# Five instead of four of the eight row pairs of the gate products by seven products, two of them with three sums of weights made in memory

## The chip, the cores and the metric

The kernel runs on one core of one Trainium2 chip. The metric is the device time of one execution in microseconds (us); the time of a kernel is the median of its runs. A run is profiled separately, and the profile's times come from that one execution. Engines are named as in the profile: PE is the matrix engine, PEld its weight loads, DVE the vector engine, ACT the scalar engine, POOL the GpSimd engine, SP the engine that issues most transfers.

## The reference

One layer of an encoder over 256 tokens of width 2048, in float32:

```python
h = rms_norm(x, attn_norm)
proj = h @ w_in
qa, ka, va, qb, kb, vb, ga, gb = jnp.split(proj, split_points, axis=-1)
ya = windowed_gqa(qa, ka, va, table, sink_a)
yb = dilated_attention(qb, kb, vb, table)
merged = sigmoid(ga) * (ya @ w_branch_a) + sigmoid(gb) * (yb @ w_branch_b)
x = x + merged @ w_out
hf = rms_norm(x, ffn_norm)
x = x + (gelu(dwconv(hf @ w_ffn_gate)) * (hf @ w_ffn_up)) @ w_ffn_down
x = x + sigmoid(rms_norm(x, ple_norm) @ w_ple_gate) * (p @ w_ple_proj)
return rms_norm(x, final_norm)
```

What matters here are `ga` and `gb`, the two gates: each is 256 tokens x 2048 columns, from 2048 rows of `w_in`. All products are made to nearly float32 exactness: every operand is split into a high and a low part of a shorter float type, and a product is three products (high x high, high x low, low x high).

## The kernel before, in words

**Blocks and pieces.** All weights are cut into 128 x 128 blocks and laid in memory in the order in which they are used (`_stream`), 16 blocks to a piece, 8 blocks (512 KB) to a load. SP issues the loads into six buffers called `raw` (L255). ACT copies a load to its high part `whi` (L278), DVE subtracts to get the low part `wlo` (L279). There are four buffers of each, so the splits run at most four ahead of PE.

**Jobs.** `_plan` lists the jobs in order: projections of the heads with the attention between them, then the gates in four quarters of the columns, then the output projection (`o`), the wide middle part (`g`, `u`, `d0`, `d1`) and the last gate (`pp`, `pgs`, `pg`). The first quarter of the gates is made plainly (`ga`, `gb`). The other three are jobs of the kind `gab`, here called gab 1, 2 and 3: each makes a quarter of `ga` and the same quarter of `gb` together, 256 tokens x 1024 columns, summing over 16 row blocks. The 16 row blocks are taken as eight pairs, 0 to 7.

**Plain pairs and pairs by seven products.** A pair is a 2 x 2 by 2 x 2 product of big blocks (two halves of the tokens, two row blocks, two groups of four column blocks). Done plainly it takes 8 products, each of three PE passes of 512 columns: 24 matmuls. Done by seven products (`seven_product`, the pairs in the second value of `_pairs`) it takes 7 x 3 = 21, but needs sums of weights and sums of the input. A plain pair is split in two parts of 8 blocks; a pair by seven products in four parts: b22 (4 blocks), two sums (8 blocks, tile `sums`), b11 and b12 (8), b22 and a third sum t4 (8). On DVE such a pair has a `wlo` of 512 elements, three of 1024, and two additions: t2 = b11 + first sum (L287), t4 = b12 + t2 (L289). A "whole" pair (`_whole`) gets its t2 ready-made from memory instead, and leaves out L287.

**Sums made in memory.** The two sums (and for a whole pair the third) of the gate and output pairs are made before their use by POOL's transfers from memory to memory, some of them adding on the way (`sums_in_memory`): for a plain set one copy of 512 KB and two additions of 256 KB (L324, L328, L329); for a whole set another copy (L327) and, after a wait, another addition (L331). `MADE_AT` lists at which job each set is asked for; POOL takes them in that order, and waits between the copies and the additions. `back` loads a set's two sums into one of two buffers `sums` (L344): the first two at job `bb` 0, each later one as soon as the split of the sums of the pair two before is done. The third sum is loaded behind the weights into the second half of a `raw` buffer (L264).

**Sums of the input.** `sums_of_input` makes the four sums of the normed input that a pair needs (ACT and DVE, `add_up`), ahead of the gab jobs.

**What sets the order.** A helper records every operation and a scheduler sets the order on each engine; `keep` pins some. `at(i, f)` ties work to a step of a job.

Of the kernel before, what the change touches and what calls it, by code (L numbers as in the profile page):

```python
# [11 lines left out]
FR = mybir.dt.float32r  # L12
# [4 lines left out]
P = 128  # L17
T = 256
D = 2048
KC = D // P  # L20
# [17 lines left out]
SUB = 8  # L38
# [81 lines left out]


TOGETHER = 3
AHEAD = 8 + 3 * 4
SAVED = 8
SPLIT = 4
ROWS = 7
SHL = 6
LATER = 4
WHOLE = (2, 3, 6, 7)
GATED = (1, 2, 3, 5)  # L130
MADE_AT = [*range(11, 34, 2), 34, 35, 36, 37, 38, 40, 42, 45]


def _pairs(kind, c):

    if kind == "pgs":
        return [0, 1, 4, 5, 2, 6, 7, 3], range(4, 8)
    if kind == "gab":
        return [0, 4, 1, 2, 6, 3, 5, 7], GATED
    if kind == "o":  # L140
        return ([2, 4, 5, 6, 7, 0, 1, 3] if c else [0, 1, 2, 4, 5, 6, 7, 3]), range(LATER, LATER + 4)
    if kind == "d1" and c == 1:
        return [5, 0, 1, 6, 2, 3, 7, 4, 8, 9, 10], range(5)
    return [8, 0, 1, 2, 3, 9, 4, 5, 6, 7, 10], range(SAVED)
# [10 lines left out]
def _stream():  # L155

    blocks = [(j[2], j[4] + k, j[3]) for k in range(KC) for j in _JOBS[:FIRST]]
    for kind, half, name, n, k0, count in _JOBS[FIRST:]:
        if isinstance(n, tuple) and len(n) == 8:
            order, seven = _pairs(kind, half)  # L160
            _EIGHT.update(range(len(blocks), len(blocks) + KC * len(order), PIECE))
            for m in order:
                if m in seven:
                    _SEVEN.append(len(blocks))
                each = [(2 * m + 1, n[4:] + n[:4]), (2 * m, n)] if m in seven else [(2 * m, n), (2 * m + 1, n)]
                blocks += [(name, k0 + k, c) for k, cs in each for c in cs]
            continue
        if kind == "gg":
            blocks += [(name, k, c) for h in range(0, KC, SUB) for c in n for k in range(h, h + SUB)]
            continue  # L170
        blocks += [(name, k, c) for k in range(k0, k0 + count) for c in (n if isinstance(n, tuple) else (n,))]
    return blocks
# [3 lines left out]
_BLOCKS = _stream()  # L176
# [4 lines left out]
def _whole(a):  # L181

    if _BLOCKS[a][0] == "w_in":
        return False
    return _BLOCKS[a][0] in ("w_out", "w_ple_gate") or (_BLOCKS[a + SUB][1] % FHALF) // 2 in WHOLE


# [19 lines left out]
def _encoder(ctx: ExitStack, tc, xt, pt, cols, table, onehot, mask, ident_in, last_gain, wts, xrows, out):  # L207
# [38 lines left out]
    held = {}  # L246
# [86 lines left out]
    def early_row():  # L333
        return ap_.tile([P, W4], F32, name="row", tag="qf", bufs=4)
# [66 lines left out]
    def wide_product(i, still, n, w, tag, places=HALVES, late=0):  # L401

        accs = [ps.tile([P, W4], F32, name="acc", tag=tag, bufs=3 if tag == "acc" else 2) for _ in places]

        def step(k, t, hi, lo):
            xh, xl = (still(k)[:, c:c + T][:, places[t]] for c in (0, T))
            acc = accs[t][:, :w * P]  # L410
            nc.tensor.matmul(acc, xh, hi, start=(k == 0), stop=False)  # L411
            nc.tensor.matmul(acc, xh, lo, start=False, stop=False)  # L412
            nc.tensor.matmul(acc, xl, hi, start=False, stop=(k == n - 1 - t * late))  # L413

        later = []
        for k in range(n):
            run_due(i, k)
            b = state["at"]
            s, o = _SUB_OF[b]
            split_to(s + 3)  # L420
            hi, lo = (m[:, o:o + w, :] for m in subs[s])
            step(k, 0, hi, lo)
            if k < n - late:
                step(k, 1, hi, lo)
            else:
                later.append((k, 1, hi, lo))
            state["at"] = b + w
            if o == _SUBS[s][1] - w:
                del subs[s]
        def rest(side=None):  # L430
            acc, c = (accs[1][:, :T], 0) if side is None else (side, T // P)
            for e, (k, t, hi, lo) in enumerate(later):
                xh, xl = (still(k)[:, c:c + T][:, places[t]] for c in (0, T))
                for i, (xs, ws) in enumerate(((xh, hi), (xh, lo), (xl, hi))):
                    nc.tensor.matmul(acc, xs, ws[:, c:c + T // P, :], start=(side is not None and e + i == 0),  # L435
                                     stop=(e + i == len(later) + 1), skip_group_check=True)
        return accs, rest
# [133 lines left out]
    def at(i, f, *a):  # L571

        due.setdefault(i, []).append((f, a))
# [7 lines left out]
    ap_ = att.enter_context(tc.tile_pool(name="att", bufs=2))  # L581
# [66 lines left out]
    b = ps.tile([NH, 2 * T], F32, name="misc")  # L648
# [222 lines left out]
    def sums_of_input(e):  # L871

        m = GATED[e]
        two = early_row().rearrange("p (k t) -> p k t", t=T)
        for k in range(2):
            nc.scalar.activation(two[:, k, :], x[:, 2 * m + k, :], AF.Copy, scale=gain(0, 2 * m + k))
        add_up(two, of_input(m))

    def of_input(m):
        e = SPLIT + 2 * GATED.index(m)  # L880
        return [held["merged"][1][:, e + c, :].rearrange("p (b n) -> p b n", n=P) for c in range(2)]

    def combined(bank, th):
# [17 lines left out]
    def row():  # L901
        return held["ff"].tile([P, W4], F32, name="row", bufs=ROWS)
# [187 lines left out]
    for i, job in enumerate(_JOBS):  # L1090
        kind, n, _, _, _, blocks = job
# [23 lines left out]

        if i in MADE_AT:
            at((i, 2), sums_in_memory, MADE_AT.index(i))
        if kind == "gab" and n > 1:
            for e in range(2):
                at((i, 5 + 6 * e), sums_in_memory, len(_SEVEN) - 4 + 2 * (n - 2) + e)  # L1120
        if kind in ("gb", "ba") and n == 0:
            for e in range(2):
                at((i, 3 + 3 * e + 5 * (kind == "gb")), sums_of_input, 2 * (kind == "ba") + e)
        if kind == "bb" and n == 0:
            for e in range(2):
                at((i, 0), back)
        if kind == "gab":
# [2 lines left out]
        if kind == "gg":  # L1130
            held["asked"] = AHEAD
        if kind == "gg" or (kind == "g" and n == FHALF):
# [60 lines left out]
        if kind == "v":  # L1193
            far = n[0] >= KVH + HG
            acc, _ = wide_product(i, stills["v"], blocks, len(n), "acc", TWINS if far else HALVES)
        elif kind in ("o", "d0", "d1", "gab", "pgs"):
            names = ("p2", "p3", "p4", "c22"), ("p1", "p5", "p6", "p7")
            places = ("sp", "sp", "pt", "pt"), ("acc", "acc", "acc", "misc")
            tags = {a: b for e in range(2) for a, b in zip(names[e], places[e ^ (n != 3 if kind == "gab" else n)])}
            still, sums_at = {"o": (stills["o"], early), "gab": (stills["ga"], of_input), "pgs": (stills["pg"], of_residual)}.get(  # L1200
                kind, (lambda k: held["act"][:, k, :], shl))
            if kind == "gab":
                if n < QUARTERS - 1:
                    th = ap_.tile([P, 2, 2, W4], F32, name="th", tag="v", bufs=1)
                    held["th", n] = {"ga": [th[:, 0, t] for t in range(2)], "gb": [th[:, 1, t] for t in range(2)]}
                else:
                    th = ap_.tile([P, 2, W4], F32, name="th", tag="s3", bufs=1)
                    held["th", n] = {"ga": [th[:, t] for t in range(2)],
                                     "gb": [ap_.tile([P, W4], F32, name="th", tag="s1", bufs=2) for t in range(2)]}
            th = held.get(("th", "pp" if kind == "pgs" else n))  # L1210
            end = kind != "d0" and n == 1
            acc = seven_product(i, *_pairs(kind, n), still, lambda m, e: [a[:, e, :] for a in sums_at(m)], tags,
                                (lambda bank: combined(bank, th)) if kind in ("gab", "pgs") else
                                (lambda bank: spread_sums(n, bank, end)))
        elif kind in stills:
            tag = {"pg": ("acc", "pt"), "pp": ("sp", "acc"), "gb": ("sp", "sp"), "ga": ("acc", "acc"),
                   "ba": ("acc", "sp" if n == 1 else "acc"), "bb": ("sp", "pt" if n == 1 else "acc")}[kind][n % 2]
            acc, rest = wide_product(i, stills[kind], blocks, 4, tag, late=8 if last else 0)
        elif kind == "gg":
            acc = products_by_halves(i, movers["g"])  # L1220
        else:
            acc = product(i, movers[kind], blocks)
# [24 lines left out]
        elif kind in ("o", "d0", "d1"):  # L1247
            parts = held["ss1" if kind == "o" else "ss2"]
            for name, t, c in (("p2", 0, 0), ("p3", 0, 1), ("p4", 1, 0), ("c22", 1, 1)):
                if end:  # L1250
                    joined(2 * n + c, t, acc[name], parts)
                else:
                    a = row()
# [63 lines left out]
```

## Time and profile before

| what | value |
|---|---|
| median of three runs | 1453.88 us (1453.02 to 1455.77) |
| the profiled execution's own time | 1452.42 us |
| its span from the first to the last instruction | 1450.6 us |
| PE busy | 1438.0 us, 99% |
| DVE busy | 1164.3 us, 80% |
| ACT busy | 852.3 us, 59% |
| gab 1, gab 2, gab 3 on PE | 368.4 to 410.9, 427.4 to 469.1, 469.1 to 509.9 us |
| POOL makes the 24 sets of sums in memory | 62.6 to about 419 us |
| the output projection `o` begins | about 543 us |

How it is read: the page's first part gives busy times; a matmul's duration in it is that of a pipelined instruction, longer than the distance between two of them. Idle time of an engine that PE doesn't wait for costs nothing. "idle before <-releaser" names what ended a wait.

### The profile page before, as it was taken

The numbers are of one execution on the slowest core, as the hardware profiler recorded it, in microseconds if no ns is written. First come the engines' busy times: TensorE is split into PE (matmuls) and PEld (weight loads), VectorE is DVE, ScalarE is ACT, GpSimd is POOL, SyncE is SP. The second block draws the span as 40 slices with busy tenths as digits, with TensorE's granted clock in tenths as the row PEclk, the third lists the DMA queues.
The fourth block names the chain that finished last, engine by engine and source line by source line (L and its number), as shares of the span: only waits on it lengthen the run. The fifth ranks groups of instructions, "written<-read, shape, count | busy, mean of one in ns | idle before, by whom it ended". The sixth has DMA issues, their size and how long they took to land.

```text
span 1450.6 us, 20823 instructions
## 1 busy us (share of the span) xinstructions
PE 1438.0 (99%) x7483; PEld 1233.8 (85%) x7483; DVE 1164.3 (80%) x1678; ACT 852.3 (59%) x1212; POOL 159.1 (11%) x242
## 2 busy tenths in 40 slices
PE   9999999999999999999999999999999999999997
PEld 8888888888888888888888888888888888888886
DVE  7687665674788878879888878997889886988895
ACT  7465544454556656666555556775555555666864
POOL 0111111211110000201111100102111100010000
PEclk9999999999999999999999999999999999999999
DMA  9799999999987668968888896989888885798672
GB/s 325 252 262 258 255 267 255 272 273 289 267 297 249 209 215 264 299 237 284 295 303 277 290 331 224 283 286 314 288 302 293 283 312 168 256 297 280 215 240 87
DMA packets 124084, 386.30 MB, mean 266 GB/s; under 512 B 14148, under 2 KB 19268, under 8 KB 123852
## 3 DMA queue, kind: packets, MB, share of 16 engines
q1 hardware_dynamic: 91932, 298.44, 60.2%
q0 software_dynamic: 30032, 82.59, 22.4%
q10 hardware_dynamic: 2016, 3.94, 1.0%
q8 instruction: 58, 0.95, 0.3%
q14 instruction: 46, 0.38, 0.1%
HBM read 354.46 MB, written 52.47 MB: 281 GB/s over the span
## 4 chain that ended last, share of the span: by engine, by line
PE 97%; DMA 1%; DVE 1%; ACT 0%; issue 0%; SPq 0%; POOLq 0%; DVEq 0%; ACTq 0%
PE acc L383 29%; PE acc L386 15%; PE acc L463 10%; PE acc L464 10%; PE acc L462 10%; PE acc L411 5%; PE acc L413 5%; PE acc L412 5%; PE first L360 2%; DMA raw<-in_wts 1%; PE pt L949 1%; PE pt L735 0%; PE acc L435 0%; ACT whi L278 0%; DVE wlo L279 0%
## 5 line engine op out<-in xcount | busy, mean ns | idle before, releaser
L279 DVE TENSOR_TENSOR wlo<-raw,whi 128x1024 fp32r<-128x1024 f32 (+2 forms) x572 | 657.0, 1165 | 124.3 <-ACT whi L278 117.8
L278 ACT ACTIVATE whi<-raw 128x1024 fp32r<-128x1024 f32 (+2 forms) x572 | 569.6, 1012 | 258.0 <-PE acc L464 86.7
L383 PE MATMUL acc<-mov,whi 128*128 128x512 f32 x1840 | 441.6, 391 | 0.0
L383 PEld LDWEIGHTS acc<-mov,whi 128*128 128x128 f32 x1840 | 337.9, 188 | 65.4
L386 PEld LDWEIGHTS acc<-mov,wlo 128*128 128x128 f32 x1840 | 237.3, 191 | 9.1 <-ACT mov L516 0.2
L386 PE MATMUL acc<-mov,wlo 128*128 128x256 f32 x1840 | 242.8, 283 | 0.0
L500 ACT ACTIVATE t<-acc 128x256 f32<-128x256 f32 x115 | 43.6, 379 | 121.3 <-PE acc L383 121.3
L411 PE MATMUL acc<-whi,mov 128*128 128x512 f32 (+1 forms) x248 | 93.6, 377 | 0.0
L413 PE MATMUL acc<-whi,mov 128*128 128x512 f32 (+1 forms) x248 | 93.5, 377 | 0.0
L412 PE MATMUL acc<-wlo,mov 128*128 128x512 f32 (+1 forms) x248 | 93.5, 377 | 0.0
L504 DVE TENSOR_TENSOR u<-acc,t 128x256 f32<-128x256 f32 x100 | 42.1, 421 | 58.4 <-ACT t L500 58.2
L462 PE MATMUL acc<-whi,act 128*128 128x512 f32 x207 | 80.8, 391 | 0.2 <-ACT whi L278 0.2
L463 PE MATMUL acc<-wlo,act 128*128 128x512 f32 x207 | 80.6, 389 | 0.0
L464 PE MATMUL acc<-whi,act 128*128 128x512 f32 x207 | 80.6, 389 | 0.0
L908 POOL DMA_DIRECT2D x<-row x36 | 30.9, 873 | 451.1 <-DMA sums<-kept 160.4
L279 DVE TENSOR_TENSOR wlo<-sums,whi 128x1024 fp32r<-128x1024 f32 x53 | 64.6, 1219 | 12.1 <-ACT whi L278 12.0
L463 PE MATMUL acc<-wlo,mov 128*128 128x512 f32 x176 | 68.5, 389 | 0.0
L464 PE MATMUL acc<-whi,mov 128*128 128x512 f32 x176 | 68.5, 389 | 0.0
L462 PE MATMUL acc<-whi,mov 128*128 128x512 f32 x176 | 68.2, 390 | 0.0
L278 ACT ACTIVATE whi<-sums 128x1024 fp32r<-128x1024 f32 x53 | 55.9, 1056 | 16.1 <-PE acc L464 9.4
L411 PEld LDWEIGHTS acc<-whi,mov 128*128 128x128 f32 x248 | 47.0, 190 | 8.7 <-DVE first L504 0.5
L413 PEld LDWEIGHTS acc<-whi,mov 128*128 128x128 f32 x248 | 47.0, 190 | 8.5
(253 smaller groups left out, 2073.2 us busy)
## 6 DMA issues: line engine op xcount, KB each, us to landing
raw<-in_wts SPq DMA_DIRECT2D x461, 512.0 KB, 5.9
sums<-kept SPq DMA_DIRECT2D x53, 512.0 KB, 5.3
kept<-in_wts POOLq DMA_DIRECT2D x60, 256.0 KB, 8.3
sums<-in_wts POOLq DMA_DIRECT2D x29, 512.0 KB, 7.6
kept<-sums POOLq DMA_DIRECT2D x29, 512.0 KB, 4.4
raw<-in_wts SPq DMA_DIRECT2D x55, 256.0 KB, 5.0
kept<-in_wts POOLq DMA_DIRECT2D x24, 512.0 KB, 9.4
x<-row POOLq DMA_DIRECT2D x36, 256.0 KB, 7.9
```

The lines of the kernel that those rows point to most:

```text
L278: nc.scalar.activation(hi, src, AF.Copy)
L279: ins = nc.vector.tensor_tensor(lo, src, hi.bitcast(F32), op=ALU.subtract)
L383: nc.tensor.matmul(acc, hi[:, k, :], m, start=(first and k == 0), stop=(last and k == SUB - 1), skip_group_check=True)
L386: nc.tensor.matmul(acc[:, T:], lo[:, k, :], m[:, :T], start=False, stop=False, skip_group_check=True)
L411: nc.tensor.matmul(acc, xh, hi, start=(k == 0), stop=False)
L412: nc.tensor.matmul(acc, xh, lo, start=False, stop=False)
L413: nc.tensor.matmul(acc, xl, hi, start=False, stop=(k == n - 1 - t * late))
L462: nc.tensor.matmul(acc, xh, hi, start=(e == 1), stop=False)
L463: nc.tensor.matmul(acc, xh, lo, start=False, stop=False)
L464: nc.tensor.matmul(acc, xl, hi, start=False, stop=(e == uses[name]))
L500: keep(nc.scalar.activation(t, acc[:, T:], AF.Copy, scale=scale))
L504: nc.vector.tensor_tensor(u, acc[:, :T], t, op=ALU.add)
```

## The change

In each gab job pair 6 is made by seven products too, so five pairs (1, 2, 3, 5, 6) and not four. The order of the pairs becomes 0, 4, 1, 2, 3, 5, 6, 7 (before: 0, 4, 1, 2, 6, 3, 5, 7). Pairs 3 and 5 become whole: their third sum is made in memory and loaded. There are 15 sets of sums for the gates and not 12, so 23 sets and not 20 in `MADE_AT` (and, as before, four for the last gate behind them). The sums of the input for pair 6 go to two tiles `fifth`, in buffers that held attention keys.

```diff
-AHEAD = 8 + 3 * 4
+AHEAD = 8 + 3 * 5
-GATED = (1, 2, 3, 5)
-MADE_AT = [*range(11, 34, 2), 34, 35, 36, 37, 38, 40, 42, 45]
+GATED = (1, 2, 3, 5, 6)
+MADE_AT = [*range(11, 34, 2), 34, 35, 36, 37, 38, 39, 40, 42, 43, 45, 46]
...
     if kind == "gab":
-        return [0, 4, 1, 2, 6, 3, 5, 7], GATED
+        return [0, 4, 1, 2, 3, 5, 6, 7], GATED
...
     if _BLOCKS[a][0] == "w_in":
-        return False
+        return _BLOCKS[a + SUB][1] // 2 in GATED[2:4]
...
     def of_input(m):
         e = SPLIT + 2 * GATED.index(m)
+        if e == KC - SPLIT:
+            return [a.rearrange("p (b n) -> p b n", n=P) for a in held["fifth"]]
...
         if kind == "bb" and n == 0:
+            held["fifth"] = [ap_.tile([P, 2 * T], FR, name="fifth", tag="kf", bufs=2) for _ in range(2)]
+            at((i, 1), sums_of_input, 4)
```

**DVE, gab 1, from the split of pair 2 on.** `wlo<-raw` and `wlo<-sums` are splits, L287 is t2, L289 is t4. Before:

```order
L279 TENSOR_TENSOR wlo<-raw,whi 128x512
L287 TENSOR_TENSOR raw<-raw,sums 128x512
L279 TENSOR_TENSOR wlo<-sums,whi 128x1024
L289 TENSOR_TENSOR raw<-raw 128x512
L279 TENSOR_TENSOR wlo<-raw,whi 128x1024 x4
L279 TENSOR_TENSOR wlo<-raw,whi 128x512
L287 TENSOR_TENSOR raw<-raw,sums 128x512
```

Now, from the end of pair 2 (pairs 3, 5 and the begin of 6):

```order
L279 TENSOR_TENSOR wlo<-raw,whi 128x512
L279 TENSOR_TENSOR wlo<-sums,whi 128x1024
L289 TENSOR_TENSOR raw<-raw 128x512
L279 TENSOR_TENSOR wlo<-raw,whi 128x1024 x2
L279 TENSOR_TENSOR wlo<-raw,whi 128x512
L279 TENSOR_TENSOR wlo<-sums,whi 128x1024
L289 TENSOR_TENSOR raw<-raw 128x512
L279 TENSOR_TENSOR wlo<-raw,whi 128x1024 x2
L279 TENSOR_TENSOR wlo<-raw,whi 128x512
L287 TENSOR_TENSOR raw<-raw,sums 128x512
L279 TENSOR_TENSOR wlo<-sums,whi 128x1024
```

The two large splits of the plain pair 6, which stood between pairs 2 and 3, are gone; the five pairs by seven products follow each other, and pairs 3 and 5 have no L287.

**SP, the loads of gab 1, from those of pair 1 on.** `kept` are sums in memory. Before:

```order
L255 DMA raw<-in_wts 128x512
L255 DMA raw<-in_wts 128x1024
L255 DMA raw<-in_wts 128x512
L255 DMA raw<-in_wts 128x1024 x2
L344 DMA sums<-kept_1431 128x1024
L255 DMA raw<-in_wts 128x1024
L255 DMA raw<-in_wts 128x512
L344 DMA sums<-kept_1620 128x1024
```

Now:

```order
L255 DMA raw<-in_wts 128x512
L255 DMA raw<-in_wts 128x1024
L255 DMA raw<-in_wts 128x512
L255 DMA raw<-in_wts 128x1024
L255 DMA raw<-in_wts 128x512
L264 DMA raw<-kept_1433 128x512
L344 DMA sums<-kept_1431 128x1024
L255 DMA raw<-in_wts 128x1024
L255 DMA raw<-in_wts 128x512
L264 DMA raw<-kept_1625 128x512
L344 DMA sums<-kept_1623 128x1024
```

The loads of pair 3 come where those of the plain pair 6 were; the sums are asked for at the same places, and each of pairs 3 and 5 has one load more (L264).

**POOL, the third set of sums (pair 3 of gab 1).** One piece of the difference:

```order
 L324 DMA kept_1431<-in_wts 128x1024
+L327 DMA kept_1433<-in_wts 128x512
 L328 DMA kept_1431<-in_wts 128x512
 L329 DMA kept_1431<-in_wts 128x512
```

Behind L329 a whole set has an L331, `kept_1433<-kept_1431`. Six of the fifteen sets of the gates are now whole, with five transfers instead of three.

## The prediction

> **What bounds the kernel now.** I read the page's chain of waits first, then the waits of PE, then the three gab jobs as stretches of time.
>
> ```profile
> span 1450.6 us, 20823 instructions
> PE 97%; DMA 1%; DVE 1%; ACT 0%; issue 0%; SPq 0%; POOLq 0%; DVEq 0%; ACTq 0%
> PE acc L462 <- ACT whi L278: 0.2, 1, 0.2
> PEld acc L463 <- DVE wlo L279: 1.8, 7, 0.5
> ```
>
> The chain that ended last is PE's own work for 97% of the span, and PE's matmuls and weight loads together waited some 2 us for the splits. So only two things move the time: the number of matmuls, and new waits of PE. The stretches of gab 1, 2 and 3 (PE, PEld, DVE, ACT, POOL busy; then clock, DMA share, GB/s):
>
> ```profile
> 368.20:410.90 42.70, 42.62 (x191) 34.52 (x190) 36.32 (x43) 23.03 (x26) 7.59 (x11) 1.00 0.99 306
> 427.20:469.00 41.80, 41.80 (x190) 34.71 (x189) 36.34 (x42) 24.20 (x27) 0.00 (x0) 1.00 0.71 228
> 469.00:509.90 40.90, 40.90 (x182) 33.87 (x181) 35.69 (x42) 26.33 (x30) 0.00 (x0) 1.00 0.70 216
> L463 PE MATMUL acc<-wlo,mov 128*128 128x512 f32 x176 | 68.5, 389 | 0.0
> 696.01 3.65 PE acc L383 x16
> ```
>
> Two readings. First, what a matmul costs: its mean is 389 ns, but matmuls overlap, and the time that one takes away from the span is the distance between starts. Sixteen of 512 columns on the chain take 3.65 us, 0.228 us each. Gab 3, with 4 x 21 + 4 x 24 = 180 matmuls and nothing else on PE, takes 40.9 us, 0.227 us each. (Gabs 1 and 2 hold eight transposes more.) Second, DVE is busy 36 us of 41 there, the nearest to PE, and in gab 1, while POOL makes sums in memory, the DMA share is 0.99; in gabs 2 and 3 POOL is done and it is 0.7.
>
> **The change, part by part.**
>
> *Removed: matmuls.* One pair in each of three jobs goes from 24 to 21: 9 matmuls x 0.227 = 2.04 us less. By their mean duration it would be 3.5 us, which the distance between starts excludes. The weight loads that go with them lie beside matmuls. The Trainium skill (TensorE: Matmul & The Clock Gate, section "Wait — 56ns, not 53.3ns?") gives 215.7 ns from start to start for 512 columns of bf16 at the full clock; by it the saving would be an estimated 1.94 us. The rows here say 227 ns, and they are used.
>
> *Moved: five such pairs in a row.* Gab 1 shows DVE going without a pause from pair 3 to pair 5:
>
> ```profile
> 393.19 0.69 DVE L279 TENSOR_TENSOR wlo<-raw,whi 128x512 fp32r<-128x512 f32 x1 [2.83 <-ACT whi L278]
> 393.80 0.69 DVE L287 TENSOR_TENSOR raw<-raw,sums 128x512 f32<-128x512 f32 x1
> 394.41 1.22 DVE L279 TENSOR_TENSOR wlo<-sums,whi 128x1024 fp32r<-128x1024 f32 x1
> 395.54 0.69 DVE L289 TENSOR_TENSOR raw<-raw 128x512 f32<-128x512 f32 x1
> 396.14 3.12 DVE L279 TENSOR_TENSOR wlo<-raw,whi 128x1024 fp32r<-128x1024 f32 x3
> 569.19 1.22 DVE L279 TENSOR_TENSOR wlo<-sums,whi 128x1024 fp32r<-128x1024 f32 x1
> 574.02 1.22 DVE L279 TENSOR_TENSOR wlo<-sums,whi 128x1024 fp32r<-128x1024 f32 x1
> 402.32 0.40 PE L462 MATMUL acc<-whi,merged 128*128 128x512 f32 x1
> 402.79 0.50 PE L463 MATMUL acc<-wlo,merged 128*128 128x512 f32 x1
> ```
>
> The last of the three splits from 396.14 is the first of pair 5 (0.68 long, so it starts at 398.58). A pair with t2 made on DVE thus takes 398.58 - 393.19 = 5.39 us of DVE; PE needs 21 x 0.227 = 4.77. A whole pair, from the output projection's run of four, takes 574.02 - 569.19 = 4.83. So DVE loses 0.62 us on PE with each plain set and 0.06 with each whole one. The last two rows show what happens when the lead is used up: PE's next matmul comes 0.47 us later instead of 0.227, a wait of 0.24 us in gab 1 today. How large the lead is after pairs 1 and 2, from gab 2:
>
> ```profile
> 442.88 1.22 DVE L279 TENSOR_TENSOR wlo<-sums,whi 128x1024 fp32r<-128x1024 f32 x1
> 444.61 5.39 DVE L279 TENSOR_TENSOR wlo<-raw,whi 128x1024 fp32r<-128x1024 f32 x5
> 446.21 0.39 PE L463 MATMUL acc<-wlo,merged 128*128 128x512 f32 x1
> ```
>
> The first of these five splits ends at 444.61 + 1.22 = 445.83, and PE uses its low part at 446.21: lead 0.38 us. Before, the plain pair 6 follows and gives the lead back. Now 3 and 5 take it to 0.26, and pair 6 with its L287 to -0.36. So PE waits 0.36 us a job, 1.1 us in all; today's 0.24 us in gab 1 is counted out. Bounds: 0, if the lead is larger than this row, and 3 x 0.62 = 1.9 us, if nothing of it is left when pair 6 begins. Pair 7 is plain and restores the lead, and the sums of products on DVE after pair 6 have the same pair 7 as cover on PE as before.
>
> *Added: loads, and longer work for POOL.* SP's load of pair 5's sums is asked for when the split of pair 2's sums ends (442.88 + 1.22 = 444.10, the SP row below). Before, the pairs 6 and 3 lay between and it had 5 us more. Now pair 3's splits begin at 444.61 + 2 x 1.22 = 447.05, pair 5's at 451.88, and the split of its sums at 452.48 on DVE, 1.06 us earlier on ACT, at 451.4. It has 7.3 us to land, 7.6 with the lead of 0.26 that is left.
>
> ```profile
> 444.12 0.33 SPq L344 DMA_DIRECT2D sums<-kept  x1
> L278 ACT ACTIVATE whi<-raw 128x1024 fp32r<-128x1024 f32 x14 | 14.8, 1060 | 18.1 <-PE acc L413 18.1
> sums<-kept SPq DMA_DIRECT2D x4, 512.0 KB, 7.7
> raw<-in_wts SPq DMA_DIRECT2D x14, 512.0 KB, 8.7
> sums<-kept SPq DMA_DIRECT2D x5, 512.0 KB, 4.2
> 62.63 0.72 POOL L324 DMA_DIRECT2D kept<-in_wts  x1
> 200.26 1.14 POOL L324 DMA_DIRECT2D kept<-in_wts  x1
> 401.05 0.81 POOL L324 DMA_DIRECT2D kept<-in_wts  x1
> 418.63 0.81 POOL L331 DMA_DIRECT2D kept<-kept  x1 [6.48 <-DMA kept<-in_wts]
> 382.75 9.68 DMA raw<-in_wts
> ```
>
> The first `sums` row is of gab 1 (368 to 412 us), the second of gabs 2 and 3 (440 to 512): 7.7 us to land with POOL's transfers beside, 4.2 without. POOL's sets stand back to back: twelve plain ones in 200.26 - 62.63 us, 11.5 each; eleven whole ones in 401.05 - 200.26, 18.3 each. The change adds three plain sets and makes six whole: 3 x 11.5 + 6 x 6.8 = 75 us, so POOL ends near 494 instead of 419. Gab 2 then lies wholly beside POOL's transfers, as gab 1 does, and gab 3 for its first half. With 7.7 us the sums are 0.1 us late; with the new L264 (256 KB) ahead of them, at gab 1's 306 GB/s 0.85 us more, 0.95 late. I take 0.5 for gabs 1 and 2 and 0.1 for gab 3: 1.1 us. Bounds: 0 with the 4.2 us, and 9.68 us (a `raw` load on the chain in gab 1), 2.1 late in each of three jobs, 6.3 us. The Trainium skill (DMA: Bandwidth & Descriptors, section "Queues, rings and completion order") says that each DMA engine goes round between the queues that have work for it. By that the second queue costs SP's load at most as much time again, an estimated 8.4 us and some 2 us of waits instead of 1.1; the trace agrees in direction (7.7 against 4.2).
>
> *Hidden.* The fifth sums of the input are four operations of 0.28 us and a low part of 512 elements (0.69, as above) on DVE, 1.8 us, and three copies on ACT. In the order they stand behind those of the fourth, where the gates' first quarter runs:
>
> ```profile
> 317.18 0.28 DVE L863 TENSOR_TENSOR row<-row 128x128 f32<-128x128 f32 x1
> L279 DVE TENSOR_TENSOR wlo<-raw,whi 128x1024 fp32r<-128x1024 f32 x14 | 17.2, 1225 | 20.2 <-ACT whi L278 20.2
> 549.97 1.45 SPq L344 DMA_DIRECT2D sums<-kept  x3
> ```
>
> From 322 to 362 us DVE sits idle 20.2 of 40 us and ACT 18.1 (row above), each before a split; without this cover it would be 1.8 us once. POOL's later end is off the path: the output projection asks for its first sums at 550, and even if all of its 25 sets up to the last one for that job took 18.3 us, it would be done at 62.6 + 25 x 18.3 = 520.
>
> *Sum:* -2.04 (matmuls) - 0.24 (today's wait) + 1.1 (DVE behind) + 1.1 (late sums) = -0.1 us on the profiled execution of 1452.42 us (1.8 of it lies around the span). That execution is 1.5 below the median of the runs, 1453.88, within their scatter; against that median the time comes to 1453.8 us.
>
> **The rivals.** A difference under 0.2%, 2.9 us, can't be told from none.
>
> *All of the saving arrives.* The lead after pairs 1 and 2 is larger than the one row of 0.38 and the sums land in time. For it: the output projection runs four whole pairs in a row with no wait of PE named in the waits above. Against: those are all whole, and here pairs 1, 2 and 6 are not. It would be -2.28 us, 1451.6: still no difference that can be told.
>
> *Slower: SP's loads fall behind POOL's for the whole of three jobs.* Place: the split of pair 5's sums in each gab. Price: lateness L a job, 3 L + 1.1 - 2.28. It decides from L = 1.4 us, that is from 9.0 us to land. For it: `raw` loads have a median of 8.7 there and one took 9.68, the DMA share is 0.99 already, and L264 is new. Against: the sums themselves land in 7.7, and gab 3 loses POOL half way. At 9.68 it is +5.1 us, 1459.0.
>
> That the change doesn't do what it says is excluded by the order of instructions: 21 matmuls for pair 6, POOL's fifteen sets, L264 in place of L287.
>
> **How the numbers follow.** The forecast has 0.54; all of the saving 0.22; slower by late loads 0.17; 0.07 remain for what I don't see, 0.04 of it a time that comes out over 0.2% below by scatter, 0.02 no difference, 0.01 slower. The forecast's own range is 1452.4 to 1455.9. The range reaches to the whole saving below, 1451.6, and above into the late loads, to L = 1.5 us a job, 3 x 1.5 + 1.1 - 2.28 = +3.3: 1451.5 to 1457.2. Faster 0.04; same 0.54 + 0.22 + 0.02 = 0.78; slower 0.17 + 0.01 = 0.18.
>
> **What would show it.** Right: PE's matmuls of a gab job are 177 and gab 3 takes 40.2 us plus its waits; PE's weight loads wait on `wlo` once a gab, in pair 6; `sums` lands in 7.5 to 8.5 us in gabs 1 and 2; POOL's last L331 near 494. Wrong: no wait of PE in the gabs (then DVE's lead was larger), waits of over 1 us at pair 5 (then the loads decide), a wait of PE in the heads' jobs before 368 us or in `o`, or gabs without POOL's transfers beside them.

## The result, and the profile after

The change makes the kernel slower: 1460.27 us median of 7 runs (1457.32 to 1469.30), against 1453.88 (1451.99 to 1455.77) of the kernel before on the same chip; the ratio of the runs is 1.0052, 95% interval 1.0039 to 1.0065. The forecast was 1453.8 us, no difference, with a range up to 1457.2. It was wrong. The runs also scatter more: 12 us instead of 4.

The profiled execution took 1457.32 us, the fastest of the seven, with a span of 1455.5 us. Its page: busy time, the DMA share in 40 slices, and the two queues that matter (q1 is SP's, q0 POOL's):

```profile
PE 1440.2 (99%) x7474; PEld 1233.0 (85%) x7474; DVE 1171.4 (80%) x1689; ACT 859.4 (59%) x1221; POOL 174.4 (12%) x263
DMA  9799999999999967978888887989888885898672
q1 hardware_dynamic: 93228, 300.80, 60.0%
q0 software_dynamic: 32672, 88.88, 24.5%
```

The same rows of the kernel before:

```profile
DMA  9799999999987668968888896989888885798672
q1 hardware_dynamic: 91932, 298.44, 60.2%
q0 software_dynamic: 30032, 82.59, 22.4%
```

The work saved is there: 7474 matmuls, 9 fewer than the 7483 before. But SP loads 300.80 MB instead of 298.44, and POOL moves 88.88 MB instead of 82.59. In the slices (36 us each) the 9s now run to the fourteenth, 509 us; before, they ended with the eleventh, at 399 us. The stretches of gab 1, of the branch products behind it and of gab 2 (PE, PEld, DVE, ACT, POOL busy; clock, DMA share, GB/s), last the branch products of the kernel before; then PE's two longest waits from gab 1 on (total, times, longest):

```profile
367.90:409.60 41.70, 41.63 (x187) 33.81 (x186) 35.99 (x41) 25.00 (x28) 8.87 (x12) 1.00 1.01 323
409.60:431.20 21.60, 18.24 (x74) 14.59 (x73) 13.39 (x17) 9.87 (x11) 5.54 (x8) 0.92 1.00 306
431.20:474.40 43.20, 42.36 (x186) 33.60 (x185) 37.62 (x45) 24.91 (x28) 7.22 (x10) 1.00 0.98 311
```

```profile
410.90:427.20 16.30, 16.30 (x73) 13.27 (x72) 11.10 (x14) 9.65 (x11) 2.06 (x3) 1.00 1.00 319
```

```profile
PE acc L411 <- DVE th L892: 3.4, 1, 3.4
PE acc L463 <- DVE wlo L279: 0.8, 1, 0.8
```

Two readings. The branch products behind gab 1 took 21.6 us for what took 16.5 before (its row stops one matmul short): there lies most of the loss, and there the mean clock is 0.92. And in gab 2 the DMA share rose from 0.71 to 0.98, with one wait of 0.8 us.

What happened behind gab 1 is seen on VectorE. The four sums of products of `combined` are L889 to L892 now (L887 to L890 before, since the change added two lines ahead); the `wlo` splits between them are of the branch weights:

```profile
408.12 0.68 DVE L889 TENSOR_TENSOR th<-acc,th 128x512 f32<-128x512 f32 x1
408.72 1.21 DVE L279 TENSOR_TENSOR wlo<-raw,whi 128x1024 fp32r<-128x1024 f32 x1
409.85 0.68 DVE L890 TENSOR_TENSOR th<-acc,th 128x512 f32<-128x512 f32 x1
412.44 1.23 DVE L279 TENSOR_TENSOR wlo<-raw,whi 128x1024 fp32r<-128x1024 f32 x1 [1.91 <-ACT whi L278]
413.59 0.68 DVE L891 SCALAR_TENSOR_TENSOR th<-acc,th 128x512 f32<-128x512 f32 x1
414.19 0.68 DVE L892 SCALAR_TENSOR_TENSOR th<-acc,th 128x512 f32<-128x512 f32 x1
```

ScalarE at the same time, and two transfers on the chain of waits (the second is of gab 2 and is used below):

```profile
411.36 1.06 ACT L278 ACTIVATE whi<-raw 128x1024 fp32r<-128x1024 f32 x1 [3.17 <-DMA raw<-in_wts]
```

```profile
401.56 9.70 DMA raw<-in_wts
...
447.89 8.87 DMA sums<-kept
```

That is the reason: a load of branch weights took 9.70 us and landed late, ScalarE waited 3.17 us for it, and the split on VectorE at 412.44 stood ahead of L891 and L892. L892 is the last reader of the bank (the place in PE's output memory) that the branch product's second accumulator needs. In the kernel before, one split less stood ahead of the last two sums:

```profile
407.96 1.21 DVE L279 TENSOR_TENSOR wlo<-raw,whi 128x1024 fp32r<-128x1024 f32 x1
409.09 0.68 DVE L888 TENSOR_TENSOR th<-acc,th 128x512 f32<-128x512 f32 x1
...
410.89 0.68 DVE L890 SCALAR_TENSOR_TENSOR th<-acc,th 128x512 f32<-128x512 f32 x1
412.76 1.22 DVE L279 TENSOR_TENSOR wlo<-raw,whi 128x1024 fp32r<-128x1024 f32 x1 [1.19 <-ACT whi L278]
```

The late split came at 412.76 there, behind the sums, and cost PE nothing. In both kernels it is the third split of branch weights behind gab 1, and in this execution it is no later than before; new in this place is that L891 and L892 stand behind it. PE in the change, behind gab 1 and in gab 2, and one stretch with its clock:

```profile
411.17 0.39 PE L412 MATMUL acc<-wlo,yab 128*128 128x512 f32 x1
414.92 0.50 PE L411 MATMUL acc<-whi,yab 128*128 128x512 f32 x1 [3.36 <-DVE th L892]
...
418.14 0.63 PE L411 MATMUL acc<-whi,yab 128*128 128x512 f32 x1
418.56 0.63 PE L412 MATMUL acc<-wlo,yab 128*128 128x512 f32 x1
...
459.23 0.50 PE L463 MATMUL acc<-wlo,merged 128*128 128x512 f32 x1 [0.76 <-DVE wlo L279]
```

```profile
418.40:420.00 1.60, 1.60 (x5) 1.23 (x5) 1.12 (x1) 0.61 (x1) 0.00 (x0) 0.56 1.02 420
```

From 411.17 to the next start at 414.92 PE lost 3.75 - 0.23 = 3.5 us. Some 1.5 us later the starts are 0.42 us apart instead of 0.227, until 419.83: eight steps of about 0.2 us more, 1.6 us. The granted clock is 0.56 in the row shown, which runs 0.2 us past the slow steps, and so about half in them. The wait thus cost 5.1 us. The Trainium skill (TensorE: Matmul & The Clock Gate, section "What's actually happening") says that the array's clock goes to half after an idle window of about 3.4 us and comes back after as long a busy one; the trace agrees, with 3.5 us lost and 3.4 us of slow steps, though a third execution (below) stays slow for 5.1 us.

In gab 2 the sums of pair 5 are late: 8.87 us to land in the chain's row above. PE's start at 459.23 comes 1.03 us late (1.26 us after the one before it), and with the three shorter delays behind it that makes 1.5 us. The median landing times of `sums` and `raw` from 368 to 474 us, gab 1 to gab 2, are now:

```profile
raw<-in_wts SPq DMA_DIRECT2D x28, 512.0 KB, 9.1
sums<-kept SPq DMA_DIRECT2D x10, 512.0 KB, 8.2
```

### The profile page after: what moved, and what is told of

Read it like the earlier page. It is cut to its first block, busy times and chain, and to the rows that moved or that the text cites. A ratio compares the mean times of both kernels' runs of the same rounds, so it can differ in the third digit from the quotient of the medians.

```text
span 1455.5 us, 20894 instructions
## 1 busy us (share of the span) xinstructions
PE 1440.2 (99%) x7474; PEld 1233.0 (85%) x7474; DVE 1171.4 (80%) x1689; ACT 859.4 (59%) x1221; POOL 174.4 (12%) x263
## 3 DMA queue, kind: packets, MB, share of 16 engines
q1 hardware_dynamic: 93228, 300.80, 60.0%
q0 software_dynamic: 32672, 88.88, 24.5%
## 4 chain that ended last, share of the span: by engine, by line
PE 94%; DMA 3%; DVE 1%; ACT 1%; issue 1%; POOLq 0%; ACTq 0%; DVEq 0%
PE acc L383 29%; PE acc L386 15%; PE acc L463 9%; PE acc L464 9%; PE acc L462 9%; PE acc L411 5%; PE acc L413 5%; PE acc L412 5%; PE first L360 3%; DMA raw<-in_wts 1%; DMA sums<-kept 1%; DVE wlo L279 1%; ACT whi L278 1%; PE pt L951 1%; PE pt L735 0%
## 5 line engine op out<-in xcount | busy, mean ns | idle before, releaser
L279 DVE TENSOR_TENSOR wlo<-sums,whi 128x1024 fp32r<-128x1024 f32 x56 | 68.3, 1219 | 13.7 <-ACT whi L278 13.5
L278 ACT ACTIVATE whi<-sums 128x1024 fp32r<-128x1024 f32 x56 | 59.1, 1055 | 18.0 <-PE acc L464 8.9
L463 PE MATMUL acc<-wlo,mov 128*128 128x512 f32 x161 | 63.0, 391 | 0.0
L464 PE MATMUL acc<-whi,mov 128*128 128x512 f32 x161 | 62.7, 389 | 0.0
L462 PE MATMUL acc<-whi,mov 128*128 128x512 f32 x161 | 62.4, 391 | 0.0
L316 POOL DMA_DIRECT2D kept<-sums x29 | 15.7, 540 | 340.6 <-DVE sums L312 238.5
L411 PEld LDWEIGHTS acc<-whi,mov 128*128 128x128 f32 x248 | 47.0, 190 | 8.7 <-DVE first L504 0.5
```

Source lines behind the costliest of these rows:

```text
L278: nc.scalar.activation(hi, src, AF.Copy)
L279: ins = nc.vector.tensor_tensor(lo, src, hi.bitcast(F32), op=ALU.subtract)
L462: nc.tensor.matmul(acc, xh, hi, start=(e == 1), stop=False)
L464: nc.tensor.matmul(acc, xl, hi, start=False, stop=(e == uses[name]))
```

## The experiments

Four theories were set against each other. A: the order on VectorE at the end of a gab is the cause. B: the transfers are: POOL's work in memory runs beside gabs 1 and 2, SP has 0.75 MB more to load in each gab (256 KB of L264 twice, and pair 6 needs 512 KB of sums, but 256 KB less of its own weights), and loads come late. C: the run of five on VectorE takes the slack that late loads would need. D: VectorE's lead alone, at the forecast's 0.36 us a gab.

All ratios are to the kernel before, run beside them.

### The sums of products ahead of the branch splits

The four sums of `combined` and the splits of the branch weights are kept in the order in which they are written:

```diff
-            if a // PIECE * PIECE in _EIGHT:
+            if a // PIECE * PIECE in _EIGHT or _BLOCKS[a][0].startswith("w_branch"):
                 keep(ins)
...
-        nc.vector.tensor_tensor(b, bank["p6"], a, op=ALU.add)
+        keep(nc.vector.tensor_tensor(b, bank["p6"], a, op=ALU.add))
...
```

> The change, with one difference: in the jobs that follow a gab job, the splits of the branch weights stand behind the four sums of products (L889 to L892) on VectorE, not between them. Theory A (order on VectorE: L892, which frees a bank for the branch product, stood behind two splits whose weights were late, and the wait of 3.4 us then cost a low clock besides): no wait of PE for th L892, the clock 1.00 there, 3.4 + 1.8 us less than the change's profile (1457.3), so 1452 to 1454 and no difference from before. Theory B (the loads themselves are late and PE meets them anyway): PE waits 2 to 4 us in the same place, for wlo instead of th, and the time stays at 1457 to 1460.

Measured: 1458.51 us, ratio 1.0030 (1.0019 to 1.0040). VectorE now does L889 to L892 with no branch split between, and L892 is done at 410.9. A wait of PE, and a transfer on the chain:

```profile
PE acc L411 <- DVE th L892: 0.2, 1, 0.2
```

```profile
485.67 9.53 DMA sums<-kept
```

The wait of the branch products for L892 is 0.2 us and the low clock is gone, as A said. But the median is only 1.8 us below that of the change (some 3 by the two ratios), not 5. PE arrives earlier in the next jobs, and meets late transfers there: in this run gab 3 has late sums (9.53 us) that gab 3 of the change had not, and loses 3.3 us against the kernel before although it has 3 matmuls fewer; POOL ends at 492 instead of 483 us. A alone falls. That a late transfer only moves to the next place is what B says, though B had put it in the same place.

### Fewer transfers: the additions for later jobs left out

```diff
+        if _BLOCKS[_SEVEN[j]][0] != "w_in":
+            return
         keep(nc.gpsimd.dma_start(two[:, :4, :], b12, accum_op=ALU.add))
```

> The change, without the additions in memory for the sums of the output projection and of the last gate (their copies stay; those two products are then wrong). POOL's transfers of these twelve sets shrink by about half and end before or in gab 1 instead of at 483 us. Theory B (POOL's transfers make SP's loads late): sums land in 4 to 5 us in gabs 2 and 3, no wait for pair 5's sums and none for L892, 1452.7 (-2.28 + 1.1). If SP's own 0.75 MB more a gab is what makes them late, or the order on VectorE alone: 1457 to 1460 with the 3.4 us wait still there.

What this kernel leaves out are the additions for the sets of the output projection and of the last gate, whose copies stay; it doesn't make the layer's result and serves to measure alone.

Measured: 1451.99 us, ratio 0.9986 (0.9977 to 0.9995). The stretches of gabs 1 and 2, the landing times from 368 to 512 us, and VectorE's last sum of products in gab 1:

```profile
368.00:410.00 42.00, 42.00 (x189) 34.22 (x188) 38.19 (x43) 25.86 (x29) 0.00 (x0) 1.00 0.73 246
427.00:469.00 42.00, 42.00 (x189) 34.24 (x188) 38.07 (x45) 27.04 (x31) 0.00 (x0) 1.00 0.75 250
```

```profile
raw<-in_wts SPq DMA_DIRECT2D x42, 512.0 KB, 5.5
sums<-kept SPq DMA_DIRECT2D x13, 512.0 KB, 4.5
```

```profile
410.79 0.68 DVE L894 SCALAR_TENSOR_TENSOR th<-acc,th 128x512 f32<-128x512 f32 x1
```

This decides most. The order of pairs, the run of five, L264, SP's 0.75 MB more and the order on VectorE are all those of the change (the last row is its L892, two lines lower, done at 411.47); only POOL's transfers are away from the gabs. PE is busy in every microsecond of the stretches, `sums` land in 4.5 instead of 8.2 us, and the kernel is 1.8 us under the one before. By themselves the order on VectorE costs nothing, and the run of five no more than the forecast had for it: PE's steps in pair 6 are too long by 0.4 us in each gab. The kernel before shows the other half: with POOL's transfers beside gab 1, but without SP's 0.75 MB more and with one split less ahead of the sums, its branch products took 16.5 us (16.3 here). So POOL's transfers alone don't cost it either. What the kernel before would gain from the same omission was not run, so the 1.8 us are not the saving alone.

### The whole sets and the fifth pair, each alone

The kernel before, with its four pairs and whole sets for pairs 3 and 5:

```diff
     if _BLOCKS[a][0] == "w_in":
-        return False
+        return _BLOCKS[a + SUB][1] // 2 in GATED[2:4]
```

> The kernel before (four pairs by seven products, its order of pairs), with the third sums of pairs 3 and 5 made in memory and loaded: six loads of 256 KB more on SP, 41 us more for POOL, L287 gone for these two pairs. Theory B (transfers): 0.5 MB more a gab beside POOL brings waits of PE of 1 to 4 us in or behind a gab, 1456 to 1459. Theory A (order on VectorE, which is that of before but for L287): no wait, 0.2 us less than before, 1453.6. By the prediction's lead of VectorE: 1453.6 as well.

Measured: 1455.20 us, ratio 1.0010 (1.0002 to 1.0019). With four pairs and one split ahead of the sums, PE still waits for the bank; then the stretch behind that wait:

```profile
PE acc L411 <- DVE th L890: 2.7, 1, 2.7
```

```profile
414.30:418.00 3.70, 3.70 (x16) 3.05 (x17) 3.05 (x5) 3.37 (x5) 0.00 (x0) 1.00 1.06 337
```

So B holds for the place and the direction with the order of the kernel before, too: `raw` loads land in 11.3 us in gab 1, against 8.7 before. The price is smaller, below the 1456 to 1459 us that B gave: 2.9 us lost there and no low clock behind it.

The change, with its five pairs and no whole set in the gabs:

```diff
     if _BLOCKS[a][0] == "w_in":
-        return _BLOCKS[a + SUB][1] // 2 in GATED[2:4]
+        return False
```

> The change with all third sums made on VectorE (L287 in all five pairs, no L264, fifteen plain sets for POOL, which then ends near 453). The lead of VectorE by the prediction: 0.38 after pair 2, then 0.62 less for each of pairs 3, 5 and 6, so PE waits 1.5 us a gab in all, 4.4 us in three; against 2.28 saved that is 1456.0 if the wait for L892 is gone too (theory B: 0.25 MB more a gab and a shorter POOL let the loads land earlier) and 1461 if it stays (theory A: the order on VectorE at the gab's end is that of the change).

Measured: 1460.44 us, ratio 1.0040 (1.0027 to 1.0053), as slow as the change and near the number that was expected if the wait for L892 stayed. POOL's last transfer is issued at 442 us. The profiled execution, at 1455.81 the fastest of its runs, has a wait of 1.5 us for L892 and several short ones for ScalarE's and VectorE's halves in pairs 3, 5 and 6 of all three gabs, 1.2 to 1.5 us in each (1.5 by the forecast's lead):

```profile
PE acc L411 <- DVE th L892: 1.5, 1, 1.5
```

What its slower runs wait for was not seen. The whole sets are thus no mistake of the change: without them POOL has less to do, and VectorE more.

### The transfers in other places, and another order of the pairs

```diff
-        if kind == "gab" and n > 1:
-            for e in range(2):
-                at((i, 5 + 6 * e), sums_in_memory, len(_SEVEN) - 4 + 2 * (n - 2) + e)
+        if kind == "u" and n == 2 * FHALF - 1:
+            for e in range(4):
+                at((i, 2 + 3 * e), sums_in_memory, len(_SEVEN) - 4 + e)
```

> The change, with the four whole sets of the last gate's weights (asked for in gabs 2 and 3, though POOL makes them as soon as it comes to them) moved in POOL's order to the last up job of the feed-forward part, where POOL is idle from 1170 us. POOL then ends near 410 us, as before the change. Theory B (POOL's transfers beside the gabs): gabs 2 and 3 are free of them, sums land there in 4 to 5 us and their waits shrink to 0.4 a gab; gab 1 keeps what it has, the wait for L892 included: 1456 to 1458. If what counts is SP's own 0.75 MB more a gab: 1459 to 1461.

Measured: 1460.34 us, ratio 1.0043 (1.0031 to 1.0056). POOL's last transfer for a set ahead of the feed-forward part is issued at 411 us. The stretch of gab 2, the wait behind gab 1, and a start of PE in the feed-forward part:

```profile
427.00:469.00 42.00, 42.00 (x189) 34.25 (x188) 36.50 (x41) 25.94 (x30) 0.00 (x0) 1.00 0.68 228
```

```profile
PE acc L411 <- DVE th L892: 3.3, 1, 3.3
```

```profile
1267.20 0.50 PE L463 MATMUL acc<-wlo,shl 128*128 128x512 f32 x1 [0.27 <-DVE wlo L279]
```

Gabs 2 and 3 are free of waits that count, as B said, and gab 1's end keeps its 3.3 us and the low clock. But the total did not fall: the feed-forward part's last product (from 1266 us) now has steps of 0.66, 0.47, 0.34 us and the like, where POOL's four sets ran until 1256 us just ahead of it. From there to the end it takes 1.9 us more than before, about the 1.8 us by which gabs 2 and 3 are shorter than in the change. The output projection takes 1.8 us more than before as well, though none of these sets runs beside it; why is open.

```diff
-        return [0, 4, 1, 2, 3, 5, 6, 7], GATED
+        return [0, 1, 2, 4, 3, 5, 6, 7], GATED
```

> The change with another order of the pairs in a gab job: the plain pair 4 stands between pairs 2 and 3 (0, 1, 2, 4, 3, 5, 6, 7), so VectorE has at most three pairs by seven products in a row; all transfers are those of the change. If VectorE's run of five takes the slack that late loads would need (theory C), the waits inside the gabs go and only the end of gab 1 remains (two splits ahead of L891 as in the change): 1455 to 1457. If the loads are late whatever the order (theory B): 1458 to 1461, with the waits now at pair 5 or 7. By the prediction's lead alone (0.36 us a gab): 1.1 us less than the change.

Measured: 1463.52 us, ratio 1.0059 (1.0041 to 1.0078). C falls as a remedy: the new order made waits of its own in pair 2 of gab 1, and the same again in gab 2. (The profiled execution is the slowest of its six, 1465.82 us.) PE, ScalarE and VectorE there:

```profile
383.20 0.50 PE L462 MATMUL acc<-whi,mov 128*128 128x512 f32 x1 [0.58 <-ACT whi L278]
```

```profile
382.09 2.96 ACT L278 ACTIVATE whi<-raw 128x1024 fp32r<-128x1024 f32 x3 [2.57 <-DVE raw L289]
```

```profile
379.55 0.69 DVE L991 SCALAR_TENSOR_TENSOR merged<-pt,merged 128x512 fp32r<-128x512 f32 x1 [1.38 <-ACT merged L990]
```

The merge of the quarter before (L990, L991) is due at the job's third and fourth step. With pair 4 second, that lay beside a plain pair; now it stands on VectorE ahead of pair 2's L289, on which ScalarE's next split waits 2.57 us. PE lost 0.3 and 0.75 us there, both in pair 2, whose last parts come late.

The next two have this order too, and are read with it; both also have the sums of products ahead of the branch splits and the last gate's sets in the feed-forward part, as above. The first holds POOL for three sets with a small multiplication that waits for the last gate value, the second does not:

```diff
+    def stop_pool(late):
+        keep(nc.gpsimd.tensor_tensor(sc.tile([P, 2], F32, name="hold"), late, mhalf[:, :2], op=ALU.mult))
...
-MADE_AT = [*range(11, 34, 2), 34, 35, 36, 37, 38, 39, 40, 42, 43, 45, 46]
+MADE_AT = [*range(11, 34, 2), 34, 35, 36, 37, 38, 39, 40, 42, 48, 49, 50]
```

> The three together, and POOL out of all gabs: order 0, 1, 2, 4, 3, 5, 6, 7, the sums of products ahead of the branch splits on VectorE, the last gate's sets in the feed-forward part, and the last three sets of the output projection held on POOL until behind gab 3 (a multiplication that waits for the last gate value). Nothing is left out. POOL works until 366 us, then from about 520 to 575. Theory B and C: no wait of PE in or behind a gab but 0.2, 2.28 us less than before: 1451.6. If SP's own loads (0.75 MB more a gab) are late without POOL: waits of 1 us and more at pair 5, 1454 or above.

> As the run before, but POOL isn't held: its transfers run beside gab 1, as before the change, and end near 410. The difference of the two is what POOL beside one gab costs. Theory B: raw weights in gab 1 land in 9 to 10 us and PE waits 1 to 3 us at its end, for wlo: 1453 to 1455. If the order on VectorE and the slack were all (theories A and C): as the run before, 1451.6.

Measured: 1463.15 us, ratio 1.0059 (1.0045 to 1.0073), with POOL out of all gabs; 1457.60 us, ratio 1.0028 (1.0019 to 1.0036), with POOL beside gab 1. The opposite of what was expected of the pair. A row of the first, whose profiled execution is the slowest of its six (1467.33 us):

```profile
566.82 0.50 PE L466 MATMUL acc<-wlo,early 128*128 128x512 f32 x1 [0.76 <-DVE wlo L279]
```

In the gabs it has only the waits of the new order, but the three sets, from 518 to 570 us, come with waits in the output projection, and the four moved ones with waits from 1271 us on; the output projection and the rest from the feed-forward part's last product on each took 4.8 us more than before. No kernel was found that does all the work and keeps the 1.8 us of the run with the additions left out: PE had waits beside POOL's sets, or just behind them, in each place where they were put.

### The change twice more, and a wait without late transfers

> The change itself, another execution with a profile (the one profiled first was the fastest of its seven, 2.95 us below their median). If the same waits only grow (theory B): the wait for th L892 of 3 us or more with the low clock behind it, and waits at pair 5 or 6 of gab 2 and now gab 1 or 3 of 1 to 2 us each, at places where sums land in over 8 us; the time 1458 to 1464. If something else than the transfers of the gabs takes the rest: the same 6.8 us of longer steps in the gabs and a difference elsewhere.

> The same, a third execution: which of the waits are the same in each (that of L892, those of VectorE's lead of 0.1 to 0.4 a gab) and which come and go (the late sums of pair 5).

Measured: 1461.01 and 1463.05 us, one execution each. PE's start behind L892 in the second of them, and the stretch behind it with its clock:

```profile
417.42 0.80 PE L411 MATMUL acc<-whi,yab 128*128 128x512 f32 x1 [3.77 <-DVE th L892]
```

```profile
417.40:423.20 5.80, 5.78 (x14) 4.58 (x15) 4.71 (x6) 3.62 (x5) 1.69 (x2) 0.50 0.93 350
```

The wait for L892 is in all three executions, 3.4, 3.1 and 3.8 us, with slow steps at the low clock behind it, for 3.4, 2.9 and 5.1 us. The late sums come and go. From PE's starts, gabs 1 to 3 took 0.5, 3.2 and 2.7 us more than those of the kernel before; with the 2.04 us that the 9 matmuls save there, that is 2.6, 5.3 and 4.7 us lost.

For the clock, two kernels with no more transfers than before; VectorE only repeats one sum of products in gab 1, three times more in the first and six in the second:

```diff
+        for _ in range(3 if th is held.get(("th", 1)) else 0):
+            nc.vector.tensor_tensor(b, bank["p6"], a, op=ALU.add)
```

> The kernel before with an artificial wait: VectorE does the first of the four sums of products of gab 1 three more times (0.6 us each, the same result), so that the one that frees the branch product's bank comes 1.8 us later. Expected: one wait of PE of 1.5 to 2 us for L892 and nothing else, the clock stays 1.00 behind it (a wait of 2.7 us in the run with four pairs and whole sets left it at 1.00): 1.8 us over the kernel before.

> The same with six more times: a wait of PE of 3.6 to 5 us. If a wait of over some 3.2 us makes the clock fall (3.4 us in the change did, 2.7 did not): eight or more matmuls of 0.43 us instead of 0.227 behind it, 1.6 us on top of the wait, 5.2 to 6.6 us over the kernel before in all, though no transfer is late. If the low clock in the change came from something else: the wait alone, 3.6 to 5.

Measured, one execution each: 1459.40 and 1461.19 us, 5.8 and 7.5 us over the 1453.65 of the kernel before beside them. The first:

```profile
415.75 0.50 PE L412 MATMUL acc<-wlo,yab 128*128 128x512 f32 x1 [0.65 <-DVE wlo L279]
419.60 0.50 PE L411 MATMUL acc<-whi,yab 128*128 128x512 f32 x1 [2.65 <-DVE th L892]
```

```profile
421.00:424.40 3.40, 3.40 (x10) 2.62 (x9) 2.69 (x3) 2.48 (x4) 0.00 (x0) 0.52 0.83 149
```

The short wait was not short: VectorE's later order made two, 0.8 and 2.8 us lost within 5 us, and the clock fell to 0.52 in the row behind them, which was not expected. The cost is 0.8 + 2.8 + 1.6 for eight slow steps = 5.2 us; the wait alone was 3.6. (The Trainium skill, TensorE: Matmul & The Clock Gate, in the section named above, speaks of one idle window of about 3.4 us; here two shorter waits with four matmuls between them were enough.) In the second kernel, too, it was not the one wait expected: three cost 0.9, 1.7 and 2.6 us, and the slow steps 2.5. So a wait made on VectorE in this place, with no transfer added, costs as much as the change lost there: that the low clock comes from the wait is shown. A single gap of 2.9 us, in the run with four pairs and whole sets, had left it at 1.00.

## Why the prediction was wrong, step by step

*Matmuls, -2.04 us:* right. There are 9 fewer, and with POOL's transfers away the kernel gained 1.8 us in the median.

*VectorE's run of five, +1.1:* right in place and in size. With POOL's transfers away PE's steps in pair 6 were too long by 0.38, 0.38 and 0.41 us in gabs 1 to 3, against 0.36 forecast. The 0.24 us of today's wait, counted out, was too small: it is one of three in gab 1 of the kernel before, 0.7 us in all with the longer step behind each.

*Late sums of pair 5, +1.1:* right in place and mechanism, too small, and too narrow. Landing in gabs 1 and 2 was forecast at 7.5 to 8.5 us and is 8.2 in the median; but the load that decides in gab 2 took 8.87 us, and late loads hit pair 6 too. The estimate of at most 8.4 us beside a second queue was passed too. Measured in gabs 1 to 3, with VectorE's share and today's wait in it, 2.6, 5.3 and 4.7 us in three executions, against 2.0 forecast for these three terms. The slower rival, which put up to 6.3 us on pair 5's sums, had the right cause and the wrong place; that its 1459.0 us lies near the median is luck.

*"The sums of products on DVE after pair 6 have the same pair 7 as cover on PE as before":* this step failed. The cover on PE is the same, but two splits of branch weights came to stand ahead of L891 on VectorE instead of one, and the second waits for a load. That load is late where the DMA share is full, 1.01 in gab 1, which the forecast read (0.99) and used only for a landing time. Either alone was free: the same order without POOL's transfers (16.3 us for the branch products), and a split as late as this one in the kernel before, behind the sums. The wait for L892 and the low clock cost 5.1, 4.7 and 6.6 us. No case of the forecast named this place, nor the clock: all three costed a wait at its own length.

*POOL's later end is off the path:* right for its jobs (483 us, forecast 494). Waits in the output projection and at its end, which the forecast listed as a sign against itself, came to 0.4 us in the first execution and 1.5 and 1.9 in the others. But they came to 1.8 us as well where POOL's last such transfer was issued at 411 us, so its later end is not shown to be their cause.

The sum by these terms for the three executions: -2.04 + 2.6 + 5.1 + 0.4 = +6.1; -2.04 + 5.3 + 4.7 + 1.5 = +9.5; -2.04 + 4.7 + 6.6 + 1.9 = +11.2. Their spans are 1455.5, 1459.2 and 1461.3 us, 4.9, 8.6 and 10.7 over the 1450.6 of before; the 0.5 to 1.2 us between lie ahead of gab 1 and behind the last matmul.

The forecast's error is one of method: it costed each late load by the landing time of a single one. Where the DMA share is 1.0 over a hundred microseconds, 2.36 MB more from SP and 6.29 MB more from POOL do not make one load later: the median of all `raw` loads went from 8.7 to 9.8 us in gab 1 and from 5.5 to 8.4 in gab 2. And PE, which the change makes faster, arrives earlier at the same loads (at the branch products at 409.6 instead of 410.9 us). Open stays why the kernel without whole sets is as slow as the change in its median, and whether the seven sets that run past 368 us fit anywhere without a loss.

## What to carry to other kernels

Where a stretch has a DMA share near 1.0, price a change by the bytes that it adds to that stretch, for every load in it, and not by the landing time of the one load that is added. Look at what stands behind a load on each engine in program order: a split that waits for a transfer holds up the sums behind it, and with them the bank that the next product needs. A wait of PE of over some 3 us, or several that add up to that within 5 us, is to be costed with the slow steps behind it.

## What the runs showed of the hardware

Behind waits that took 3.3 us or more from PE in one piece, or 3.6 us in two pieces within 5 us, the granted clock was 0.50 to 0.56 in the rows shown, and 512-column matmuls started 0.43 us apart instead of 0.227 for 2.9 to 5.1 us; behind a wait of 2.9 us the clock stayed at 1.00. From gab 1 on, SP's 512 KB loads landed in 8.2 to 9.1 us in the median beside POOL's sums in memory, and in 4.5 to 5.5 without. Of the change the seven executions lay within 12 us; 26 of the kernel before, beside the first four experiments, lay within 3.5, and 17 beside the next four within 5.7.
